# Expert layer of a decoder block: products with u kept on chip and gated from PSUM, v rows of two token tiles summed on TensorE strips

## The chip, the cores and the metric

The kernel runs on one core of a Trainium2 chip. A core has five engines that work side by side, each through its own instructions in order: TensorE (PE, matrix products into PSUM), VectorE (DVE), ScalarE (ACT), GpSimd (POOL) and SyncE (SP, which here only issues transfers). Sixteen DMA engines move data between DRAM and the on-chip memory SBUF; POOL issues the gathers by index, SP the plain transfers. The metric is the time of one execution in microseconds, the median of several runs.

## The reference

A block of a decoder with 512 tokens of 1024 values. Two token mixers (a gated linear recurrence and a dilated window attention) are merged and added to x; behind them comes the expert layer, which this change is about:

```python
def peer_ffn(x, w_q, sub_keys, u, v):
    q = (x @ w_q).reshape(B, S, PEER_HEADS, 2, PEER_HALF)
    s = jnp.einsum('bshpc,hpnc->bshpn', q, sub_keys)
    s1, i1 = lax.top_k(s[..., 0, :], PEER_TOPK)
    s2, i2 = lax.top_k(s[..., 1, :], PEER_TOPK)
    ...                                   # the best 16 of the 256 sums of each head
    gate = jax.nn.softmax(top_s, axis=-1)
    def block(args):
        xb, ib, gb = args
        hid = jnp.einsum('thkd,td->thk', u[ib], xb)
        a = jax.nn.gelu(hid, approximate=False) * gb
        return jnp.einsum('thk,thkd->td', a, v[ib])
```

Each token picks 128 of 16384 experts (8 heads of 16). For each picked expert the token's product with a row of u goes through gelu and a gate, and weighs a row of v; u and v have 16384 rows of 1024 float32 values, 67 MB each.

## The kernel before

The 512 tokens are four tiles of 128. The mixers run by halves (`Front(0)` for tiles 0 and 1, `Front(1)` for 2 and 3). `routing(T, rq)` finds a tile's 128 experts per token and their gates. The expert layer then reaches u and v in two ways.

*By gathering.* Tiles 0 and 3 (`UG`) gather their rows of u: for pair number j, one indirect transfer brings 128 rows, one for each token, and DVE reduces their product with the tokens' vector (L626, in `u_steps`). A tile needs 128 such gathers of 512 KB. Tile 3 also gathers its rows of v, and DVE adds each, weighted, to an accumulator (L645, in `v_steps`). The pool `gat` has three places for gathered rows (`row`), and two more (`rq`) take some of the later ones.

*By streaming.* Tiles 1 and 2 (`UD`) meet all of u: `hidden(b)` loads one of 128 blocks of 128 experts (`ub`), splits it into a high and a low part (`uh` on ACT, `ul` on POOL or DVE) and makes 24 products with 256 tokens (L109), then gelu. Tiles 1, 2 and 0 (`VD`) meet all of v in the last loop: block b's activations (`Gc`, split into `ah` and `al`) and its rows of v (`vb`, split into `vh` and `vl`) give 18 products of 128 x 512 (L834).

For the streamed tiles the gates have to be spread: `scatter_steps` builds from the pairs' two key numbers, by comparisons (`e12`, L666) and products (`eg`, L670) on DVE and small matrix products (L680), a 128 x 128 table of gates for each token, four tokens in a group. ACT copies it into `Gx`, and it goes to DRAM (`g_d`) ordered by tokens and comes back (`Gc`) by blocks. For tile 0 the scattered weights already hold gelu and gate; for tiles 1 and 2 the products with u are multiplied in when a block is used (L825).

The order of the work: the program's text gives priorities, and a scheduler orders each engine's instructions from them with its own model of time. Two pumps (`rows` and `scat`) put steps of gathering and scattering between other work, so many to a unit. 46 hidden blocks (`NPRE`) run ahead of the products with v; the other 82 run between them, in a ring of 58 places.

Of the kernel before, what the change touches and what calls it, by code (L numbers as in the profile page):

```python
# [18 lines left out]
P = 128  # L19
# [49 lines left out]
def kernel(ctx: ExitStack, tc: tile.TileContext, x, wst, par, cst, cols, g2, keys, u, v, ut, vr, out):  # L69
# [28 lines left out]
    def accumulate(out, ws, xs, cut, w_stays):  # L98
        """Sum over the blocks of w x, in three products where they come in two parts."""
# [24 lines left out]
    # lower bound: softmax over the two logit rows, row 0  # L124
# [5 lines left out]
    # values of the first group by token; of the other two with every fourth token's in a row  # L130
# [13 lines left out]
    class Front:  # L144
        """The mixers of one half of the tokens, and the queries of their expert layer."""

        def __init__(self, h, hi_pool, after_unit):
# [5 lines left out]
            for t in range(NT):  # L153
# [5 lines left out]
                for c in range(0, KC, 4):  # L159
# [20 lines left out]
        def slot(self, i, ks=slice(0, KC)):  # L180
            """Row blocks ks of a slot's weights, UK of them in a tile: the blocks' operands in order."""
# [14 lines left out]
        def proj(self, i, x, T):  # L196
            """A slot's 256 columns of the half's products with x, on the partitions (T) or along them."""
# [112 lines left out]
        def proj_attn(self):  # L310
# [47 lines left out]
            # with the scores' scale of 1 / 8  # L358
# [69 lines left out]
        def proj_gates(self):  # L428
# [6 lines left out]
            # behind the last exponential: the functions' tables take turns  # L435
# [5 lines left out]
        def post(self):  # L441
            """Merge, output projection, second norm and expert queries."""
# [22 lines left out]
            for b in range(4):  # L465
# [13 lines left out]
            for t in range(NT):  # L479
# [21 lines left out]
                # x1 waits in the output rows it belongs to  # L501
# [17 lines left out]
    def route_bank(T):  # L519
        pt = pvg.tile([P, 512], F32, name="vg") if T == 3 else pr.tile([P, 512], F32, name="pr")  # L520
# [11 lines left out]
    def routing(T, rq):  # L532
        """Top 16 of the 256 sums of the two halves' top 16.  A pair (a, b) has (a+1)(b+1)-1 pairs before it that
        are no worse, so only those with (a+1)(b+1) <= 16 can be among them."""
# [64 lines left out]
        if T in VD:  # L599
            pt = route_bank(T)  # L600
# [302 lines left out]
```

## Time and profile before

| | |
|---|---|
| time, median of 3 runs (lowest to highest) | 1847.26 us (1845.63 to 1848.25) |
| the profiled execution, first to last instruction | 1845.0 us |
| busy: PE, DVE, ACT, POOL | 91%, 78%, 43%, 43% |
| DMA, mean over the span | 475.61 MB, 258 GB/s |
| gathers by index | 384 of 512 KB |

The profile shows one execution. Busy times are shares of the span; a PE that is busy need not be at its peak, since products overlap in the array and each is shown with its whole way through it. A product of plain float32 shows as two records, one of the split operands (`uh`, `vh`, ...) as one. The granted clock is a share of TensorE's full speed, 1.00 or 0.50 at a time. The profiled execution's span is 2.3 us under the median.

### The profile page before, as it was taken

The page shows a single profiled execution, that of the slowest core. Times are in us where ns is not written, and L with a number is a line of the kernel's source. Part 1 is how long each engine was busy: PE and PEld are TensorE (multiplying, and loading weights), DVE is VectorE, ACT ScalarE, POOL GpSimd, SP SyncE. Part 2 cuts the span into 40 slices and gives each one's busy share as a digit, 9 for nine tenths or more (in the row PEclk, how much of TensorE's full clock was granted, in tenths as well). Part 3 has the DMA queues.
Part 4 walks back from the last instruction along what each step waited for, and adds up shares of the span by engine and source line. Part 5 has one row for each costly group of instructions (what it writes and reads, how often), then busy time and mean ns, then how long its engine had stood idle before and what let it go on. Part 6 is the DMA issues. An engine that isn't in the chain of part 4 may idle for free.

```text
span 1845.0 us, 28370 instructions
## 1 busy us (share of the span) xinstructions
PE 1674.0 (91%) x10573; PEld 1482.8 (80%) x10573; DVE 1444.1 (78%) x2681; ACT 795.6 (43%) x1348; POOL 793.6 (43%) x546
## 2 busy tenths in 40 slices
PE   6999889889789989888867899999999999999987
PEld 6998888667667878777867878888888888888766
DVE  5644547887887758999999977877877788888777
ACT  5655551211114556368756534343343434343232
POOL 3211312463664335556566543344323464444442
PEclk9999999988899989889978899999999999999999
DMA  6453553778787887534455799999988999999887
GB/s 196 153 158 119 175 194 118 270 235 276 244 279 264 297 298 261 183 111 145 152 183 202 238 372 334 339 328 326 367 298 299 345 339 341 340 340 317 288 309 278
DMA packets 169963, 475.61 MB, mean 258 GB/s; under 512 B 14304, under 2 KB 62688, under 8 KB 168800
## 3 DMA queue, kind: packets, MB, share of 16 engines
q1 hardware_dynamic: 112416, 270.56, 43.0%
q0 software_dynamic: 55296, 201.35, 30.9%
q10 hardware_dynamic: 2112, 1.88, 0.3%
q8 instruction: 83, 1.36, 0.3%
q14 instruction: 56, 0.46, 0.1%
HBM read 443.85 MB, written 28.84 MB: 256 GB/s over the span
## 4 chain that ended last, share of the span: by engine, by line
PE 47%; DVE 25%; DMA 11%; issue 9%; POOL 5%; ACT 1%; DVEq 0%; POOLq 0%; SPq 0%; ACTq 0%
PE acc L834 19%; PE pp L109 13%; PE ph L109 10%; DMA row<-in_u_dram,idx 6%; DVE row L626 4%; DVE e L666 4%; DVE eg L670 3%; POOL row L618 3%; DMA Gc<-g_d 3%; PE pg L680 2%; PE pr L680 1%; DVE cs L564 1%; DVE rest L515 1%; DVE ti L514 1%; DVE h2g L645 1%
## 5 line engine op out<-in xcount | busy, mean ns | idle before, releaser
L618 POOL DMA_INDIRECT row<-in_u_dram,idx x206 | 254.9, 1237 | 383.8 <-DVE row L626 274.3
L626 DVE SCALAR_TENSOR_TENSOR row<-row,h2g 128x1024 f32<-128x1024 f32 x206 | 272.4, 1328 | 62.2 <-DMA row<-in_u_dram,idx 61.3
L109 PE MATMUL ph<-hH,uh 128*128 128x256 f32 x1024 | 302.1, 295 | 7.1 <-ACT pre L792 6.0
L109 PE MATMUL ph<-hH,ul 128*128 128x256 f32 x1024 | 302.9, 296 | 5.0 <-POOL ul L95 5.0
L109 PE MATMUL ph<-hL,uh 128*128 128x256 f32 x1024 | 299.0, 292 | 0.0
L834 PE MATMUL acc<-vl,ah 128*128 128x512 f32 x768 | 241.8, 396 | 9.3 <-DVE vl L95 9.3
L834 PE MATMUL acc<-vh,al 128*128 128x512 f32 x768 | 240.0, 393 | 0.0
L94 ACT ACTIVATE uh<-ub 128x1024 fp32r<-128x1024 f32 x128 | 136.7, 1068 | 230.7 <-PE ph L109 214.1
L834 PE MATMUL acc<-vh,ah 128*128 128x512 f32 x768 | 222.5, 395 | 9.9 <-ACT vh L94 9.9
L109 PEld LDWEIGHTS ph<-hH,uh 128*128 128x128 f32 x1024 | 205.9, 201 | 12.8 <-ACT pre L792 7.8
L109 PEld LDWEIGHTS ph<-hH,ul 128*128 128x128 f32 x1024 | 205.5, 201 | 6.3 <-POOL ul L95 5.8
L109 PEld LDWEIGHTS ph<-hL,uh 128*128 128x128 f32 x1024 | 204.6, 200 | 3.8
L680 PEld LDWEIGHTS <-e 128*128 128x128 bf16 x1152 | 124.8, 119 | 73.4 <-DVE eg L670 65.4
L834 PEld LDWEIGHTS acc<-vl,ah 128*128 128x128 f32 x768 | 143.2, 190 | 40.0 <-DVE vl L95 11.8
L834 PEld LDWEIGHTS acc<-vh,ah 128*128 128x128 f32 x768 | 142.9, 190 | 38.2 <-ACT vh L94 10.5
L834 PEld LDWEIGHTS acc<-vh,al 128*128 128x128 f32 x768 | 145.5, 190 | 31.8
L94 ACT ACTIVATE ah<-Gc 128x384 fp32r<-128x384 f32 x128 | 66.9, 523 | 229.4 <-PE acc L834 226.7
L95 DVE TENSOR_TENSOR vl<-vb,vh 128x1024 fp32r<-128x1024 f32 x128 | 156.1, 1219 | 12.2 <-ACT vh L94 12.0
L618 POOL DMA_INDIRECT row<-in_v_dram,idx x76 | 111.6, 1469 | 120.0 <-DVE h2g L645 109.2
L680 PE MATMUL pg<-eg,e 128*128 128x128 bf16 x768 | 103.1, 297 | 51.8 <-DVE eg L670 51.3
L94 ACT ACTIVATE vh<-vb 128x1024 fp32r<-128x1024 f32 x128 | 135.6, 1059 | 28.6 <-DMA vb<-in_vr_dram 27.9
L674 ACT ACTIVATE eg<-e,pk 128x128 bf16<-128x128 bf16 x320 | 115.4, 565 | 70.9 <-DVE e L666 68.1
(279 smaller groups left out, 3582.4 us busy)
## 6 DMA issues: line engine op xcount, KB each, us to landing
w<-in_wst_dram SPq DMA_DIRECT2D x140, 512.0 KB
ub<-in_ut_dram SPq DMA_DIRECT2D x128, 512.0 KB
vb<-in_vr_dram SPq DMA_DIRECT2D x128, 512.0 KB
Gc<-g_d SPq DMA_DIRECT2D x15, 1536.0 KB
g_d<-Gx SPq DMA_DIRECT2D x16, 960.0 KB
g_d<-Gx SPq DMA_DIRECT2D x8, 1024.0 KB
row<-in_u_dram,idx POOLq DMA_INDIRECT x206
sc<-in_x_dram SPq DMA_DIRECT2D x4, 512.0 KB
```

What stands on the lines that cost most here:

```text
L94: nc.scalar.activation(hi, x, AF.Copy)
L95: (eng or nc.vector).tensor_tensor(out=lo, in0=x, in1=hi.bitcast(F32), op=ALU.subtract)
L109: nc.tensor.matmul(out, l, r, start=(i == 0), stop=(i == len(ops) - 1))
L514: nc.vector.max_index(out=ids[:, 0:8], in_max=vals[:, 0:8], in_values=src)
L515: nc.vector.match_replace(out=rest[:, :w], in_to_replace=vals[:, 0:8], in_values=src, imm_value=-BIG)
L618: nc.gpsimd.indirect_dma_start(out=r, out_offset=None, in_=src, in_offset=bass.IndirectOffsetOnAxis(ap=index, axis=0))
L626: nc.vector.scalar_tensor_tensor(r, r, 1.0, h2g[T], op0=ALU.mult, op1=ALU.mult, accum_out=hid[:, g, j:j + 1])
L666: nc.vector.tensor_tensor(out=e12, in0=iota[:, None].to_broadcast([P, 2, NKEY, GS]), in1=e[:, 0:2].to_broadcast([P, 2, NKEY, GS]), op=ALU. ...
L670: last_e2[0] = nc.vector.tensor_tensor(out=eg[:, :n], in0=e12[:, 1:2].to_broadcast([P, n, NKEY, GS]), in1=e[:, 2:2 + n].to_broadcast([P, n ...
L674: nc.scalar.activation(eg[:, 2, :, q], e12[:, 1, :, q], AF.Copy, scale=pk3[:, VD.index(T), i + k + q:i + k + q + 1])
L680: nc.tensor.matmul(pt[:, q], e12[:, 0, :, q0 + q], eg[:, j, :, q0 + q], start=(j == 0), stop=(j == 2))
L834: nc.tensor.matmul(acc[t][c], lt, r[:, c * 512:(c + 1) * 512], start=(b == 0 and i == 0), stop=(b == NKEY - 1 and i == 2))
```

## The change

Tile 0 leaves the streamed products with v: `VD` is gone, and the last loop has 12 products a block instead of 18, for tiles 1 and 2. Tiles 0 and 3 gather their rows of v, 256 gathers in place of 128. These now run by token: `idxT` holds the transposed indices, a gather brings the 128 rows of v of one token, and PE sums them with the token's weights: a column of weights stands in a strip of zeros (`wz`), so that a product of 32 columns adds one token's row to its place in PSUM (L653 of the new kernel). Tokens 32 apart go to the four strips of the array (`tile_position`), and a step of `v_steps` gathers two rows.

All 128 hidden blocks are done before the scatter, and their gelus stay in SBUF (`hid_all`, two tiles of 64 blocks). The scatter, now for tiles 1 and 2 only, multiplies its table from PSUM right onto them (L690 of the new kernel); `Gx`, `g_d`, `Gc` and the pump `scat` are gone. Then the products with v follow. The loads of u have two places instead of three, those of v four, in the places of `hH` and `hL`; gathered rows have five places in turn (`row_places`), from the second half's mixers on. POOL makes the low part of 16 blocks of u instead of 46.

```diff
 UG = (0, 3)
 UD = (1, 2)
-VD = (1, 2, 0)
...
+ROWS_F, ROWS_U, ROWS_S, ROWS_V = 3, 1.25, 1.5, 1.2
...
+        if T in UG:
+            nc.tensor.transpose(pt[:, 0], full, ident)
+            nc.vector.tensor_copy(idxT[:, UG.index(T)], pt[:, 0])
...
     def v_steps(T):
         g = UG.index(T)
-        acc = const.tile([P, D], F32, name="h2g")
-        for j in range(P):
-            r = row(idx[:, g, j:j + 1], v, j % 5 < 2)
...
-                nc.vector.scalar_tensor_tensor(acc, r, hid[:, g, j:j + 1], acc, op0=ALU.mult, op1=ALU.add)
-            yield 1
+        av = aT[:, g].rearrange("p (c m) -> p c m", c=NR)
+        acc = [pv.tile([P, 512], F32, name=f"pv{c}") for c in range(2)]
+        for m in range(RQ):
+            w = wz[m % len(wz)]
+            nc.scalar.activation(w[:, :, RQ - 1:RQ], av[:, :, m:m + 1], AF.Copy)
+            for c0 in range(0, NR, 2):
+                cc = range(c0, c0 + 2)
+                rs = [row(idxT[:, g, c * RQ + m:c * RQ + m + 1], v) for c in cc]
+                for h in range(2):
+                    for c, r in zip(cc, rs):
+                        nc.tensor.matmul(acc[h][c * RQ:(c + 1) * RQ], w[:, c, RQ - 1 - m:2 * RQ - 1 - m],
+                                         r[:, h * 512:(h + 1) * 512], start=(m == 0), stop=(m == RQ - 1),
+                                         tile_position=(0, c * RQ))
+                yield 2
+        finish(T, acc)
...
-                    nc.scalar.activation(Gx[:, :, k + q0:k + q0 + 4].rearrange("p i t -> p t i"), pt, AF.Copy)
...
-            nc.sync.dma_start(out=g_d[:, gi, k0:], in_=Gx[:, k0:])
...
+        t0 = ti * P + k
+        for i, a in enumerate(hid_all):
+            at = a[:, :, t0:t0 + GS]
+            nc.vector.tensor_mul(at, pt[:, :, i * HB:(i + 1) * HB].rearrange("p t i -> p i t"), at)
...
-    gat = ctx.enter_context(tc.tile_pool(name="gat", bufs=3, side="left", **TILE))
+    gat = ctx.enter_context(tc.tile_pool(name="gat", bufs=2, side="left", **TILE))
...
+    row_places = [(gat, "row", 2)] * 2 + [(rx, "rowx", 3)] * 3
...
+        for b in range(HB, NKEY):
+            hidden(b)
+            rows(ROWS_U)
+
+    with tc.tile_pool(name="gb", bufs=1, side="right", **TILE) as gb, \
+            tc.tile_pool(name="pg", bufs=3, space=PSUM, side="right", **TILE) as pg:
+        for k in range(0, P, GS):
+            for ti in range(len(UD)):
+                scatter(ti, k)
+                rows(ROWS_S)
...
     for b in range(NKEY):
-        if b % GB == 0:
...
-                nc.sync.dma_start(out=Gc, in_=g_d[:, :, b:b + GB])
-        a = pre[b]
-        gsl = Gc[:, :, b % GB]
-        nc.vector.tensor_mul(gsl[:, :ngu], a.rearrange("p (g t) -> p g t", t=GT), gsl[:, :ngu])
+        a = hid_all[b // HB][:, b % HB]
...
-        for t in range(len(VD)):
+        for t in range(len(UD)):
...
-        if b + NPRE < NKEY:
-            hidden(b + NPRE, ph)
-        rows(ROWS_D)
+        rows(ROWS_V)
```

Where the scheduler puts the instructions. First DVE behind the mixers, while the routings of the last tiles run. Before, the scatter's comparisons (`e`) and products (`eg`) stand between the routing's steps:

```order
L666 TENSOR_TENSOR e_6829<-iota,pk 128x1024
L551 CAST tf<-ti 128x128
L513 MAX sv<-cs 128x8 x4
L585 TENSOR_REDUCE idf<-sel 128x16
L670 TENSOR_TENSOR eg<-e_6829,pk 128x1024
L552 TENSOR_SCALAR tf<-tf 128x4x16
L514 MAX_INDEX si<-sv,cs 128x8
```

Now, at the same part of a routing, the subtractions `ul` and the products of gathered u rows (`row`, `rq`, `keys_sb` are their places) stand there:

```order
L92 TENSOR_TENSOR ul<-ub,uh 128x1024
L629 SCALAR_TENSOR_TENSOR keys_sb,hid<-keys_sb,h2g 128x1024
L629 SCALAR_TENSOR_TENSOR rq,hid<-rq,h2g 128x1024
L577 TENSOR_TENSOR eq<-iota,sf 128x800
L92 TENSOR_TENSOR ul<-ub,uh 128x1024
L629 SCALAR_TENSOR_TENSOR rq,hid<-rq,h2g 128x1024
L582 TENSOR_REDUCE idf<-sel 128x16
L629 SCALAR_TENSOR_TENSOR row,hid<-row,h2g 128x1024 x2
```

What moved: the scatter left this stretch of DVE, and between the first step of routing 3 and the transposing of tile 3's weights 140 products with u rows and 46 subtractions came in.

Then PE in the second half of the hidden blocks. Before, hidden products (`ph`) stood between the products with v (`acc00` to `acc21` are three tiles by two halves of the columns):

```order
L834 MATMUL acc10_9808<-vh_15453,ah_15447 128x512
L834 MATMUL acc11_9809<-vh_15453,ah_15447 128x512
L834 MATMUL acc20_9810<-vh_15453,ah_15447 128x512
L834 MATMUL acc21_9811<-vh_15453,ah_15447 128x512
L109 MATMUL ph_14355<-hH_68,uh_14351 128x256
L109 MATMUL ph_14355<-hL_69,uh_14351 128x256
```

Now the strips (`pv0` and `pv1` are the two halves of the columns) stand between the hidden products:

```order
L653 MATMUL pv0_6180<-row_11154,wz0_3086 32x512
L653 MATMUL pv1_6181<-row_11154,wz0_3086 32x512
L653 MATMUL pv0_6180<-rq_11156,wz0_3086 32x512
L653 MATMUL pv1_6181<-rq_11156,wz0_3086 32x512
L653 MATMUL pv0_6180<-rq_11186,wz1_3087 32x512
L653 MATMUL pv1_6181<-rq_11186,wz1_3087 32x512
L106 MATMUL ph_8910<-hH_68,uh_8906 128x256
L106 MATMUL ph_8910<-hL_69,uh_8906 128x256
L653 MATMUL pv0_6180<-keys_sb_11188,wz1_3087 32x512
L653 MATMUL pv1_6181<-keys_sb_11188,wz1_3087 32x512
L106 MATMUL ph_8910<-hH_68,ul_8907 128x256
```

What moved: the two halves of one row, which are one strip of the array, stand side by side, and the row of the next strip often only after some hidden products. Of the 256 rows of v, 24 stand among the first 62 hidden blocks, 145 among the other 66 (100 runs of strips, 71 of a single row, three of five rows) and 87 among the scatter (25 runs); none is left for the last loop.

Last, DVE in the scatter, where nothing else is left on it (`hid` with its numbers are the two tiles of gelus):

```order
L674 TENSOR_TENSOR e_11616<-iota,pk 128x1024
L678 TENSOR_TENSOR eg<-e_11585,pk 128x1024
L678 TENSOR_TENSOR eg<-e_11616,pk 128x1024
L690 TENSOR_TENSOR hid_5554<-pg,hid_5554 128x64x4
L690 TENSOR_TENSOR hid_8474<-pg,hid_8474 128x64x4
L674 TENSOR_TENSOR e_11648<-iota,pk 128x1024
```

What moved: the scatter is a stage of its own, behind all hidden blocks and ahead of all products with v, and two products from PSUM came to each group.

## Rows read from the trace of the kernel before

**Rows 1.** Windows: length; PE, PEld, DVE, ACT, POOL busy; clock; DMA share; GB/s.

```profile
0.00:295.00 295.00, 268.48 (x2305) 254.40 (x2306) 154.24 (x259) 152.47 (x250) 63.89 (x32) 0.98 0.50 157
295.00:690.00 395.00, 348.95 (x1899) 288.06 (x1898) 312.66 (x862) 121.48 (x265) 184.06 (x149) 0.91 0.78 263
690.00:1075.00 385.00, 311.73 (x2276) 293.25 (x2275) 359.25 (x773) 234.57 (x434) 226.98 (x139) 0.88 0.57 192
1075.00:1835.00 760.00, 744.33 (x4096) 646.96 (x4095) 615.67 (x787) 287.10 (x403) 318.65 (x227) 0.99 0.92 328
```

**Rows 2.** The page, part 3: queue, packets, MB, share of 16 engines' span.

```profile
q1 hardware_dynamic: 112416, 270.56, 43.0%
q0 software_dynamic: 55296, 201.35, 30.9%
```

**Rows 3.** The chain that ended last: start, duration in us, what, how many.

```profile
412.88 7.51 DMA row<-in_u_dram,idx
719.91 2.87 PE pr L680 x24
1113.24 4.13 PE acc L834 x18
1126.00 2.84 PE ph L109 x24
```

**Rows 4.** Lines 666 and 670 by source: shortest, median and longest in ns.

```profile
L666 DVE TENSOR_TENSOR e<-iota,pk x96: 660/686/3107, 567.5 to 1044.1; 128x1024 bf16<-128x1024 bf16 x96
L670 DVE TENSOR_TENSOR eg<-e,pk x96: 664/684/5904, 575.9 to 1047.0; 128x1024 bf16<-128x1024 bf16 x80, 128x1536 bf16<-128x1536 bf16 x16
```

**Rows 5.** Windows on lines 666, 670, 626 and 95, in this order.

```profile
295.00:690.00 395.00, 17.45 (x24) 0.91 0.78 263
690.00:1075.00 385.00, 86.33 (x72) 0.88 0.57 192
...
295.00:690.00 395.00, 17.08 (x23) 0.91 0.78 263
690.00:1075.00 385.00, 85.95 (x74) 0.88 0.57 192
...
295.00:690.00 395.00, 149.31 (x216) 0.91 0.78 263
690.00:1075.00 385.00, 63.26 (x88) 0.88 0.57 192
1075.00:1835.00 760.00, 126.35 (x208) 0.99 0.92 328
...
690.00:1075.00 385.00, 14.11 (x12) 110.92 (x44) 0.88 0.57 192
```

**Rows 6.** Timeline of PE: start, us, instruction; plain float32 products, full and in strips.

```profile
670.66 3.19 PE L109 MATMUL pp<-vs,w 128*128 128x256 f32 x14
...
556.21 1.12 PE L386 MATMUL pt<-kT,vs 64*32 64x128 f32 x16
557.26 0.79 PE L109 MATMUL pp<-hT,w 128*128 128x256 f32 x1
```

**Rows 7.** Windows around these products: the granted clock is third from the end.

```profile
556.00:558.00 2.00, 2.00 (x19) 1.19 (x19) 2.00 (x4) 0.00 (x0) 1.70 (x2) 0.50 0.27 33
671.00:673.50 2.50, 2.50 (x14) 2.19 (x13) 0.34 (x1) 1.49 (x2) 0.00 (x0) 1.00 1.03 416
```

**Rows 8.** Groups by line and form: count, busy us, mean ns, idle before.

```profile
L95 DVE TENSOR_TENSOR ul<-ub,uh 128x1024 fp32r<-128x1024 f32 x82 | 101.1, 1233 | 53.7 <-ACT uh L94 51.6 <-ACT ah L94 1.2 <-issue 0.7
L825 DVE TENSOR_TENSOR Gc<-pre,Gc 128x256 f32<-128x256 f32 x128 | 44.6, 417 | 45.2 <-DMA Gc<-g_d 45.2
L454 DVE TENSOR_TENSOR pairA<-pp,pairA 128x512 f32<-128x512 f32 x8 | 5.5, 686 | 6.6 <-PE pp L109 6.6
```

**Rows 9.** Waits from 295 to 690 us: in total, times, the longest.

```profile
POOL row L618 <- DVE row L626: 98.7, 36, 24.4
DVE row L626 <- DMA row<-in_u_dram,idx: 48.6, 33, 5.2
```

More of the change, by code (lines that the diff above doesn't have):

```diff
@@ L519, in route_bank @@
     def route_bank(T):
-        pt = pvg.tile([P, 512], F32, name="vg") if T == 3 else pr.tile([P, 512], F32, name="pr")
+        pt = pr.tile([P, 512], F32, name="pr")
         return pt.rearrange("p (n k) -> p n k", k=NKEY)
@@ L631, in u_steps @@
[L631 to L635 removed]
+            nc.scalar.activation(hid, hid, AF.Gelu)
+            nc.vector.tensor_mul(hid, hid, gates[:, T])
+            pt = pvg.tile([P, 512], F32, name="vg")
+            nc.tensor.transpose(pt[:, :P], hid, ident)
+            nc.vector.tensor_copy(aT[:, g], pt[:, :P])
@@ new lines, in scatter @@
+    def scatter(ti, k):
+        e = pk[:, ti, :, None, k:k + GS]
+        e12 = gb.tile([P, 2, NKEY, GS], BF16, name="e12", bufs=2)
+        nc.vector.tensor_tensor(out=e12, in0=iota[:, None].to_broadcast([P, 2, NKEY, GS]),
+                                in1=e[:, 0:2].to_broadcast([P, 2, NKEY, GS]), op=ALU.is_equal)
+        eg = gb.tile([P, 3, NKEY, GS], BF16, name="eg", bufs=2)
+        n = 2 if k // GS % 4 < ACT3 else 3
+        nc.vector.tensor_tensor(out=eg[:, :n], in0=e12[:, 1:2].to_broadcast([P, n, NKEY, GS]),
+                                in1=e[:, 2:2 + n].to_broadcast([P, n, NKEY, GS]), op=ALU.mult)
+        if n == 2:
+            for q in range(GS):
+                nc.scalar.activation(eg[:, 2, :, q], e12[:, 1, :, q], AF.Copy, scale=pk3[:, ti, k + q:k + q + 1])
+        pt = pg.tile([P, 512], F32, name="pg").rearrange("p (n k) -> p n k", k=NKEY)
+        for q in range(GS):
+            for j in range(3):
+                nc.tensor.matmul(pt[:, q], e12[:, 0, :, q], eg[:, j, :, q], start=(j == 0), stop=(j == 2))
+        t0 = ti * P + k
+        for i, a in enumerate(hid_all):
+            at = a[:, :, t0:t0 + GS]
+            nc.vector.tensor_mul(at, pt[:, :, i * HB:(i + 1) * HB].rearrange("p t i -> p i t"), at)
@@ L760 @@
     routing(1, rq1)
-    pr_bank = lambda: pr.tile([P, 512], F32, name="pr")
-    scat.add(scatter_steps(1, pr_bank))
     f.hgrn(0)
@@ L771 @@
         rows(2 * P)
-        scat(P)
     fctx.close()
-    dp = ctx.enter_context(tc.tile_pool(name="dp", bufs=1, side="right", **TILE))
-    us = ctx.enter_context(tc.tile_pool(name="us", bufs=2, side="right", **TILE))
-    pre = []
-    Gcs = [dp.tile([P, NGT, GB, GT], F32, name="Gc")]
-    nc.sync.dma_start(out=Gcs[0][:, :P // GT], in_=g_d[:, :P // GT, :GB])
-    def hidden(b, pool):
-        dst = dp.tile([P, NU], F32, name="pre", bufs=RING)
-        pre.append(dst)
-        ub = us.tile([P, KC, P], F32, name="ub", bufs=3)
+    pv = ctx.enter_context(tc.tile_pool(name="pv", bufs=1, space=PSUM, side="right", **TILE))
@@ L791, in hidden @@
         accumulate(pt, [tuple(a[:, k] for a in ubs) for k in range(KC)], (hH, hL), slice(None), True)
-        nc.scalar.activation(dst, pt, AF.Gelu)
-    with tc.tile_pool(name="php", bufs=2, space=PSUM, side="right") as php, \
-            tc.tile_pool(name="pg", bufs=3, space=PSUM, side="right") as pg:
-        pg_bank = lambda: pg.tile([P, 512], F32, name="pg")
-        routing(2, rq2)
-        scat.add(scatter_steps(0, pg_bank))
-        scat.add(scatter_steps(2, pg_bank))
-        scat(P)
-        for b in range(NPRE):
-            hidden(b, php)
-        routing(3, rq3)
@@ L804 @@
-    h2g[3] = const.tile([P, D], F32, name="h2g")
-    nc.sync.dma_start(out=h2g[3], in_=h2_d)
-    rows.add(u_steps(3))
-    with tc.issue_after(last_e2[0].ins):
-        rows(4)
-    rows.add(v_steps(3))
-    rctx.close()
-    ph = ctx.enter_context(tc.tile_pool(name="ph", bufs=1, space=PSUM, side="left", **TILE))
-    vs = ctx.enter_context(tc.tile_pool(name="vs", bufs=2, side="left", **TILE))
+        nc.scalar.activation(hid_all[b // HB][:, b % HB], pt, AF.Gelu)
+    v0 = v_steps(0)
+    rows.add(itertools.islice(v0, ROWS_V0 // 2))
@@ new lines @@
+    rows.add(u_steps(3))
+    rows.add(v0)
+    rows.add(v_steps(3))
+    with tc.tile_pool(name="us", bufs=2, side="right", **TILE) as us, \
+            tc.tile_pool(name="php", bufs=3, space=PSUM, side="right", **TILE) as php:
+        routing(3, rq3)
+        routing(2, rq2)
+        h2g[3] = const.tile([P, D], F32, name="h2g")
+        nc.sync.dma_start(out=h2g[3], in_=h2_d)
+        for b in range(HB):
+            hidden(b)
+            rows(ROWS_U)
+        rctx.close()
+        row_places[2:] = [(rq_pool, "rq", 2)] * 2 + [(rq_pool, "keys_sb", 1)]
+        hb = ctx.enter_context(tc.tile_pool(name="hb", bufs=1, side="left", **TILE))
+        hid_all.append(hb.tile([P, HB, NU], F32, name="hid1"))
+        for b in range(HB, NKEY):
+            hidden(b)
+            rows(ROWS_U)
@@ L835 @@
                                      start=(b == 0 and i == 0), stop=(b == NKEY - 1 and i == 2))
-        if b + NPRE < NKEY:
-            hidden(b + NPRE, ph)
-        rows(ROWS_D)
+        rows(ROWS_V)
     rows(2 * S)
-    for t, T in enumerate(VD):
-        x1r = gat.tile([P, D], F32, name="row")
-        nc.sync.dma_start(out=x1r, in_=out[T * P:(T + 1) * P])
-        for c in range(2):
-            cs = slice(c * 512, (c + 1) * 512)
-            nc.vector.tensor_add(x1r[:, cs], acc[t][c], x1r[:, cs])
-        nc.sync.dma_start(out=out[T * P:(T + 1) * P], in_=x1r)
+    for t, T in enumerate(UD):
+        finish(T, acc[t])
```

121 lines of the change are left out of this document (44 added, 77 removed).

## The prediction

> **What bounds the kernel now.** I read the windows by stage first. The profiled execution spans 1845.0 us (the median of the runs is 2.3 us above it), and it falls into four stages with different limits [rows 1]. To 295 us: the first half's mixers, PE busy 268 of 295. From 295 to 690: the second half's mixers with gathers of u beside them; no engine is full (PE 349, DVE 313 of 395), DMA at 0.78. From 690 to 1075: DVE busy 359 of 385, so DVE sets the pace, in a stage with the 46 hidden blocks that run ahead and 72 of the 96 groups of the scatter [rows 5]. From 1075 to 1835: PE busy 744 of 760 and DMA at 0.92 and 328 GB/s, both nearly full. The last 10 us store. So the 91% of PE in the table above is an average, and what PE could deliver is read from the chain: a block of 18 products with v takes 4.13 us, 0.229 each, and a block of 24 hidden products 2.84 us, 0.118 each [rows 3]. In the last stage 128 x 4.13 = 529 and the remaining 82 blocks x 2.84 = 233 give 762: that stage is PE at its peak, hardly a wait in it.
>
> The waits of the second stage show why it is loose: POOL waited 98.7 us for DVE to give back a place of a gathered row, and DVE 48.6 us for rows to land [rows 9]. A gather stands in the chain with some 7.5 to 8 us [rows 3]; three places allow no more.
>
> **The change, stage by stage.** I name the new stages A to G. A load is 524 kB (128 x 1024 x 4), gathered or streamed.
>
> A, the first half, keeps its order on every engine: **295**.
>
> B, the second half. Scatter leaves it: 17.5 + 17.1 us of DVE [rows 5]. Nine more rows come in (117 stand there, 108 did: 216 entries, two a row) at 149.3 / 108 = 1.38 us [rows 5]: +12. DVE falls from 313 to 291. On POOL it is the next gather that stands behind a place not yet given back, and DVE's products with u wait for that. Five places instead of three should take most of the 48.6 us; I take three quarters, so the 82 us of DVE idleness become 46. 291 + 46 = 337 is the lower end, 395 (nothing gained) the upper. 263 GB/s x 395 = 104 MB need 301 us at full rate (below), so transfers would not forbid it; at 0.9 full they seldom come without waits. I take **350**.
>
> C, the hidden blocks as long as u rows of tile 3 are reduced on DVE. The new order has 62 hidden blocks on PE up to the transposing of tile 3's weights, and on DVE both routings, 140 row products and 46 subtractions ul. From the old third stage: 359.3 - 86.3 - 86.0 (scatter) - 63.3 (rows) - 14.1 (halves) = 110 us are the routings and small things [rows 1, 5]. The rows cost 140 x 1.30; that is between 63.3 / 44 = 1.44 in that stage and 126 / 104 = 1.21 in the last [rows 5]. So 182, the subtractions 46 x 1.233 = 57 [rows 8]: 349. What lies between the median and the longest of the same scatter instruction (0.686 and 3.107 us [rows 4]) is worth a look: 72 of them took 1.20 on average here. It is the stage in which POOL runs subtractions of 110.9 / 44 = 2.5 us [rows 5], and those are 16 instead of 46 now. I add 30 for what is left of that. PE needs 62 x 2.84 = 176, transfers (62 + 152 rows) 112 MB. DVE ran at 93% in the old stage: 349 to 400, I take **380**.
>
> D, the other 66 hidden blocks, with 145 rows of v on PE. This is where the change is dear. One row is two products of 32 x 512, each in full float32. No such product is in the trace. Its bounds: a 128x256 float32 product shows as two records, and 14 records ran in 3.19 us at full clock. One alone takes 0.79 at half clock, some 0.39 at full; (3.19 - 0.39) / 13 = 0.215 from one to the next [rows 6, 7]. So 512 columns take 0.43 a record, and a row four records, 1.72 us, if nothing overlaps. Narrow strips do overlap: 16 records of 128 columns in 32-wide strips started at 556.21, and the next full product at 557.26, at a granted clock of 0.50 [rows 6, 7]. In series they would take 16 x 0.215 = 3.44 (half the columns at half the clock), they took 1.05, so four strips ran together, less 0.19 for draining. But the order on PE undoes the pairing: both halves of one row go to the same strip, and the scheduler puts hidden products between one row and the next. 100 runs of strips stand in D, 71 of them a single row. A run costs at least 1.72, and three runs of five rows cost twice that: 177 us; in series all 145 rows cost 249. The row is near the first, so I take 177. Each run begins and ends with a change of shape: 0.19 on leaving by the row above (at half clock), somewhat less at full; I take 0.25 for both, 25 us. 66 x 2.84 = 187. Sum 389, transfers 211 loads, 111 MB. In-order waits for rows come on top: **405**, bounds 365 and 470.
>
> The Trainium skill, "TensorEngine Tiling", Key Properties, says that changing the tiling mode drains the engine, while tiles of one mode run in parallel. The gap at 557.26 agrees. By parallel tiles alone D would be 365, by the drain at each of the 199 changes it is the sum above.
>
> E, the scatter by itself, 64 groups. DVE: e12 0.686, eg 0.684 [rows 4], or 1.03 where it has 1536 elements instead of 1024 (one of four), and two products from PSUM of 256 elements, 0.417 each if they run like the one from SBUF, 0.686 each if the scattered reading costs as much as twice the elements [rows 8]. 2.29 to 2.83 a group, 147 to 181 us. PE: 12 x 0.119 [rows 3] = 1.43 a group, 25 runs of strips with 52 us, 150 in all. The 87 rows: five places, a cycle of 7.5 us in flight and some 3 us of issue and use, 2.1 a row, 183. Three limits close together: **185**, bounds 160 and 260 (the latter with strips at half clock, as at 556).
>
> F, the products with v, now for two tiles and with nothing beside them: 12 x 0.229 = 2.74 a block, 351, with the first load **355**. DVE, 616 of 760 us busy there before [rows 1], loses u's rows, v's sums and ul from this stage; transfers are 67 MB. G, the end: **10**.
>
> Taken out at no cost: the 50 MB of gates through DRAM (25 MB written and read; transfers were full only where PE was too), DVE's accumulation of v, ACT's copies to Gx. They are hidden by PE in the old last stage; where PE is no cover (the third stage) they are counted above.
>
> Sum: 295 + 350 + 380 + 405 + 185 + 355 + 10 = 1980, against 1845; with the 2 us to the median **1982**. PE is given 351 instead of 529 us of products with v, but 250 of strips, and the work that once lay under PE's last stage, the scatter and u's rows on DVE, now stands before it in line.
>
> **Rivals.** *Slower still: strips do not overlap.* If runs go in series, D rises to 470 and E, with 150 us of strips, to 250: about 2110. The 16 records speak against it; that two halves of one row share a strip speaks for some of it. The same price comes if the clock drops: the old third stage had 0.88 [rows 1].
>
> *B gains nothing*, since transfers or the mixers' own order hold it: 2027. For it: 0.78 of DMA already.
>
> *Faster: C and D run at the pace of transfers.* 297 rows and 128 blocks are 223 MB. Full rate by the queues: 270.6 MB in 43.0% and 201.4 MB in 30.9% of 1845 us [rows 2], 341 and 353, taken as 346 GB/s: 644 us instead of 785. That gives 1841, and it decides from there: C and D must stay under 650 us together. For it: the old last stage ran 760 us at 0.92. Against it: the least counts, 349 on DVE and 365 on PE, are 714 one after the other, and the order on each engine lets neither overlap.
>
> The Trainium skill, "DMA: Bandwidth & Descriptors", Bandwidth, puts the limit of HBM at about 358 GB/s for each core and that of the fabric, for a core alone, at 435. The queues' 346 agree with the first. By the second, at 425 as measured there, the transfers of C and D would take 524 us, and this rival would come to 1721.
>
> **How the numbers follow.** The sum (1900 to 2060) 0.70; strips in series or clock down (2060 to 2200) 0.13; between the sum and the transfers' pace (1851 to 1900) 0.10; transfers' pace or better 0.07, of which 0.02 within 0.2% (3.7 us, about what a measurement of this kernel tells from nothing) and 0.05 faster. All lower ends together give 1869, all upper ends 2194. From 1875 to 2100 leaves out less than 2 in 10.
>
> **What would show it.** Right: hidden products that begin by 650; DVE over 90% busy to about 1025, then under 30% for 400 us while PE is full with strips of 0.8 us in chain; a scatter stage of 160 to 260 us; a last stage of 128 blocks at 2.74 with DMA near 0.55. Wrong: D under 340, which would mean strips overlapping across hidden products; a second half still of 395; a C in which DVE waits for rows.

## The result, and the profile after

The changed kernel takes **2040.3 us** (median; 2030.7 to 2041.9) against 1847.2: a ratio of 1.1044, 95% interval 1.1019 to 1.1068. The forecast was slower, 1982 us, 1875 to 2100. The profiled execution spans 2028.9 us. Its windows, cut where the named stages end in this trace (for each engine busy us and instructions, then the granted clock as a share of 2.4 GHz, the DMA share and GB/s):

```profile
0.00:295.00 295.00, 268.59 (x2307) 254.47 (x2308) 154.30 (x260) 152.76 (x250) 64.44 (x34) 0.97 0.48 157
295.00:645.00 350.00, 314.30 (x1705) 257.15 (x1703) 311.67 (x921) 76.67 (x160) 219.59 (x171) 0.97 0.88 316
645.00:1028.00 383.00, 273.65 (x1622) 231.87 (x1622) 327.52 (x752) 94.42 (x143) 275.33 (x199) 0.83 0.83 293
1028.00:1447.00 419.00, 403.65 (x2162) 233.69 (x2163) 80.64 (x71) 95.25 (x167) 149.97 (x141) 1.00 0.76 261
1447.00:1673.00 226.00, 197.71 (x1125) 110.75 (x1117) 129.40 (x258) 73.94 (x216) 86.68 (x86) 0.90 0.65 219
1673.00:2029.00 356.00, 350.21 (x1536) 289.49 (x1536) 213.40 (x261) 187.41 (x254) 0.00 (x0) 0.99 0.60 186
```

| stage | forecast | measured |
|---|---|---|
| A, first half | 295 | 295 |
| B, second half | 350 | 350 |
| C, hidden blocks beside u rows | 380 | 383 |
| D, hidden blocks beside v strips | 405 | 419 |
| E, scatter | 185 | 226 |
| F and G, products with v, end | 365 | 356 |
| span | 1980 | 2029 |

Where [rows 1] had one stage with PE and DMA both full, there are now three in line, each with room on a different engine: PE in C (274 of 383 us busy), DVE in D (81 of 419), transfers in F (0.60). The chain that ended last in D (followed back from the last instruction through what released each one), by line:

```profile
by line: PE ph L106 45.2%; PE pv L653 42.5%; DMA keys_sb<-in_v_dram,idxT 6.2%; issue 2.4%; ACT uh L91 2.2%; POOL rq L621 0.9%; DVE ul L92 0.3%; POOL row L621 0.2%; ACT wz L647 0.1%; ACTq L91 0.0%; POOLq L621 0.0%; ACTq L647 0.0%
```

Of 419 us that is 189 of hidden products (forecast 187), 178 of strips (forecast 177) and 26 of waits for a row. PE's timeline in D shows what a run of strips costs, that is, strips with no other product between them (start, us, count; x8 is two rows, x4 one):

```profile
1240.20 1.92 PE L653 MATMUL pv<-rq,wz 128*32 128x512 f32 x8
1242.05 0.39 PE L106 MATMUL ph<-hH,uh 128*128 128x256 f32 x1
1242.27 0.28 PE L106 MATMUL ph<-hL,uh 128*128 128x256 f32 x1
1242.48 1.91 PE L653 MATMUL pv<-keys_sb,wz 128*32 128x512 f32 x4
1244.31 0.39 PE L106 MATMUL ph<-hH,ul 128*128 128x256 f32 x1
```

Two rows cost what one costs: 1.85 us to the next hidden product against 1.83. Over all records of D, 100 runs hold 144 rows and take 210 us from first strip to next product: 2.1 us a run. The Trainium skill, "TensorEngine Tiling (Array Packing)", Key Properties, has tiles of one mode working in parallel and a drain at a change of mode; the trace agrees with the first (1.85 beside 1.83), and the second is small here (four records of 0.43 are 1.72 of the 1.83).

### The profile page after: what moved, and what is told of

It reads as the page before. It is cut to its first block, busy times and chain, and to the rows that moved or that the text cites. A ratio compares the mean times of both kernels' runs of the same rounds, so it can differ in the third digit from the quotient of the medians.

```text
span 2028.9 us, 27909 instructions
## 1 busy us (share of the span) xinstructions
PE 1808.1 (89%) x10446; PEld 1377.4 (68%) x10446; DVE 1216.9 (60%) x2515; ACT 680.4 (34%) x1189; POOL 796.0 (39%) x630
## 4 chain that ended last, share of the span: by engine, by line
PE 60%; DVE 18%; DMA 7%; issue 6%; POOL 5%; ACT 1%; DVEq 0%; POOLq 0%; ACTq 0%
PE acc L836 17%; PE pv L653 13%; PE ph L106 12%; PE pp L106 12%; DVE rowx L629 5%; PE pg L686 3%; DVE row L629 2%; DMA rowx<-in_u_dram,idx 2%; DMA keys_sb<-in_v_dram,idxT 2%; POOL row L621 2%; DMA row<-in_v_dram,idxT 1%; DVE ul L92 1%; DVE rest L512 1%; DVE rq L629 1%; DMA w<-in_wst_dram 1%
## 5 line engine op out<-in xcount | busy, mean ns | idle before, releaser
L92 DVE TENSOR_TENSOR ul<-ub,uh 128x1024 fp32r<-128x1024 f32 x112 | 138.3, 1248 | 335.8 <-ACT uh L91 335.6
L653 PE MATMUL pv<-row,wz 128*32 128x512 f32 x416 | 181.4, 603 | 5.3 <-DMA row<-in_v_dram,idxT 4.9
L621 POOL DMA_INDIRECT row<-in_v_dram,idxT x104 | 109.6, 1054 | 183.3 <-PE pv L653 149.2
L791 ACT ACTIVATE hid<-ph 128x256 f32<-128x256 f32 x128 | 48.6, 379 | 367.7 <-PE ph L106 367.6
L621 POOL DMA_INDIRECT rowx<-in_u_dram,idx x110 | 137.5, 1250 | 74.6 <-DVE rowx L629 30.5
L629 DVE SCALAR_TENSOR_TENSOR rowx<-rowx,h2g 128x1024 f32<-128x1024 f32 x110 | 150.8, 1377 | 22.4 <-DMA rowx<-in_u_dram,idx 18.1
L621 POOL DMA_INDIRECT row<-in_u_dram,idx x102 | 125.4, 1230 | 90.3 <-DVE row L629 57.4
L629 DVE SCALAR_TENSOR_TENSOR row<-row,h2g 128x1024 f32<-128x1024 f32 x102 | 139.8, 1375 | 31.1 <-DMA row<-in_u_dram,idx 31.1
L621 POOL DMA_INDIRECT rq<-in_v_dram,idxT x92 | 98.7, 1073 | 122.2 <-PE pv L653 107.9
L653 PE MATMUL pv<-rq,wz 128*32 128x512 f32 x368 | 142.4, 599 | 3.6 <-DMA rq<-in_v_dram,idxT 3.6
L836 PE MATMUL acc<-vh,ah 128*128 128x512 f32 x512 | 138.0, 391 | 1.0 <-ACT ah L91 1.0
```

Source lines behind the costliest of these rows:

```text
L92: (eng or nc.vector).tensor_tensor(out=lo, in0=x, in1=hi.bitcast(F32), op=ALU.subtract)
L621: nc.gpsimd.indirect_dma_start(out=r, out_offset=None, in_=src, in_offset=bass.IndirectOffsetOnAxis(ap=index, axis=0))
L629: nc.vector.scalar_tensor_tensor(r, r, 1.0, h2g[T], op0=ALU.mult, op1=ALU.mult, accum_out=hid[:, j:j + 1])
L653: nc.tensor.matmul(acc[h][c * RQ:(c + 1) * RQ], w[:, c, RQ - 1 - m:2 * RQ - 1 - m], r[:, h * 512:(h + 1) * 512], start=(m == 0), stop=(m = ...
L791: nc.scalar.activation(hid_all[b // HB][:, b % HB], pt, AF.Gelu)
L836: nc.tensor.matmul(acc[t][c], l[:, t * P:(t + 1) * P], r[:, c * 512:(c + 1) * 512], start=(b == 0 and i == 0), stop=(b == NKEY - 1 and i = ...
```

## Experiments

Beside each median stands its ratio to the kernel before, run on the same chip.

**Pairs.** Hold the four products of two rows together, to see whether the order of strips is D's price.

```diff
+                (c, r), (c1, r1) = zip(cc, rs)
+                first = strip(c1, r1, 0)
+                with tc.issue_after(first.ins):
+                    strip(c, r, 0)
+                    strip(c1, r1, 1)
+                    strip(c, r, 1)
```

> The four products of a pair of v rows are held together on PE, the later row's first. Read from the changed kernel: 71 runs of one row took 1.83 us each, 16 runs of two rows 1.85 as well. Theory (strips of two rows overlap when they stand together, and PE sets the pace beside the hidden blocks): the stage with 64 hidden blocks and 107 rows has 64 x 2.84 + 54 x 1.85 = 282 us of PE and takes 290 to 330 instead of 419; the 32 rows that the order moves into the last stage add 16 x 1.85 = 30 there; the kernel comes to 1935 to 1975. Rival (row places and landing pace the rows, PE only waits inside its strips): rows go on at the 2.9 us that 145 rows took in 419 us, the stage takes 107 x 2.9 = 310 but PE is idle in a fifth of it, the scatter stage stays at 226, and with longer waits for the second row of each pair the kernel stays above 1990.

1967.5 us, 1.0654 (1.0626 to 1.0682). The window of D:

```profile
1045.00:1350.00 305.00, 290.40 (x1970) 205.77 (x1970) 78.29 (x66) 91.55 (x153) 120.57 (x107) 0.99 0.84 295
```

50 runs for 107 rows now, 100 us: again 2.0 a run, 0.93 a row instead of 1.46. PE is still busy 290 of 305 us and the kernel is under 1990, as the first theory has it; the length alone would not tell, since the rival had 310. Not all of D's 114 us are gained: 37 rows fewer stand in it, and the last stage, which got 33 of them, took 385 instead of 356. The chain of this D goes through gathers and their places, no longer through products:

```profile
by line: issue 40.5%; DMA rq<-in_v_dram,idxT 21.3%; DMA keys_sb<-in_v_dram,idxT 14.9%; POOL rq L621 7.3%; POOL row L621 6.3%; POOL keys_sb L621 3.2%; PE ph L106 3.0%; DMA row<-in_v_dram,idxT 2.0%; PE pv L652 1.3%; POOLq L621 0.3%; PE vg L63
```

So the price of a run is shown, and the row places come close behind it.

**Strips undone.** v rows gathered by pair number again, one row for each token, as before the change (the expectation's "by token" is a slip), and summed on DVE; all else of the change stays.

```diff
+            r = row(idx[:, g, j:j + 1], v)
+                nc.vector.scalar_tensor_tensor(acc, r, hid[g][:, j:j + 1], acc, op0=ALU.mult, op1=ALU.add)
```

> The strips undone: v rows are gathered by token, as before the change, and summed on DVE with one scalar_tensor_tensor each, for both tiles; gates from PSUM, products kept on chip, row places and everything else as changed. Theory (strips on PE are the dear part, 2.0 us of PE for a row where DVE has 340 us idle beside the last 66 hidden blocks): that stage has 159 rows x 1.35 + 67 x 1.28 = 300 us of DVE, 66 x 2.84 = 187 of PE and 226 loads, 118 MB, 342 us; it takes 330 to 360 instead of 419; the stage ahead grows by some 15 rows (400), the scatter has 129 + 66 x 1.35 = 218 us of DVE and takes 225 to 245, the last stage 355: 1965 to 2005. Rival (where a row is summed matters little, because transfers and row places pace the rows): no stage moves by over 15 us, 2025 to 2055.

1929.7 us, 1.0437 (1.0395 to 1.0479), lower than the range, mostly by E. D and E:

```profile
1032.00:1371.00 339.00, 250.02 (x1606) 235.68 (x1606) 279.05 (x230) 92.16 (x135) 221.50 (x159) 0.85 0.95 349
1371.00:1574.00 203.00, 101.11 (x768) 83.67 (x768) 202.08 (x322) 73.04 (x196) 79.41 (x68) 0.51 0.57 184
```

D runs at the transfers' rate (349 GB/s, 0.95), E has DVE busy throughout. More than half of the loss, 111 of 193 us, is what summing on strips costs over summing on DVE. The 349 stands beside the 358 GB/s for a core that the Trainium skill gives ("DMA: Bandwidth & Descriptors", Bandwidth).

**Three places in B.** Rows go round three places until the mixers end, then five.

```diff
-    row_places = [(gat, "row", 2)] * 2 + [(rx, "rowx", 3)] * 3
+    row_places = [(gat, "row", 2)] * 2 + [(rx, "rowx", 3)]
...
+    row_places[2:] = [(rx, "rowx", 3)] * 3
     fctx.close()
```

> Rows gathered in the second half's mixers go round three places instead of five; five again from the hidden blocks on. Theory (the second half fell from 395 to 350 us because five places took away waits for rows): hidden blocks begin 30 to 50 us later, at 675 to 695, and since the order moves the rest of tile 0's u rows beside the hidden blocks, that stage grows too; 2055 to 2100 for the kernel. Rival (the second half is shorter because the scatter's work left it): hidden blocks begin within 10 us of 645, DVE's waits for rows in that stage stay near the 26 us that they have now, and the kernel is within 15 us of 2040.

2055.7 us, 1.1120 (1.1089 to 1.1150): at the low edge of the theory's total, but not by its mechanism, and neither side whole. The first hidden products, of the changed kernel, of this one, and of the kernel before (first and last start behind the durations), and DVE's largest wait in this one's B:

```profile
L106 PE MATMUL ph<-hH,uh x1024: 277/282/582, 644.9 to 1445.3; 128*128 128x256 f32 x171
```
```profile
L106 PE MATMUL ph<-hH,uh x1024: 274/282/582, 651.0 to 1441.1; 128*128 128x256 f32 x171
```
```profile
L109 PE MATMUL ph<-hH,uh x1024: 274/281/582, 687.1 to 1718.5; 128*128 128x256 f32 x171
```
```profile
DVE row L629 <- DMA row<-in_u_dram,idx: 48.2, 25, 6.2
```

The 48.6 us of [rows 9] are back, and hidden products still begin at 651. So the two places gave 6 of the 42 us from 687 to 645, and moved 22 rows (106 to 128) into B. The rest came with what else the change took out of it. The scatter is the likely part: beside its 35 us on DVE it held PE, in B of the kernel before, for 34 us (first PE, then PEld; its products' line 680), and PE's busy time there fell from 349 to 314:

```profile
295.00:690.00 395.00, 33.80 (x264) 30.03 (x264) 0.91 0.78 263
```

No run puts the scatter alone back, so this is argued, not shown.

**Half of u's products.**

```diff
+            n = D // 2 if T else D
+            nc.vector.scalar_tensor_tensor(r[:, :n], r[:, :n], 1.0, h2g[T][:, :n], op0=ALU.mult, op1=ALU.mult,
```

> Leaves out half of the product with u for tile 3: DVE multiplies and sums 512 of 1024 columns of each gathered row; the gathers are whole. Theory of the prediction (the first 62 hidden blocks stand under DVE's row products): DVE loses 128 x 0.65 = 83 us of the 328 that it is busy in that stage, which falls from 383 us to the transfers' 325 to 340; the kernel comes to 1980 to 2005. Rival (five row places and the way of a gather, not DVE, set 2.5 us a row): the stage stays at 370 to 385, and the kernel at 2025 to 2045.

2046.4 us, 1.1085 (1.1038 to 1.1133). C alone:

```profile
653.00:1011.00 358.00, 268.00 (x1601) 224.99 (x1602) 266.77 (x747) 93.03 (x141) 243.37 (x198) 0.85 0.87 309
```

DVE lost 61 us and C 25: neither theory whole. DVE sets part of C's pace; what holds the other part is not shown (no engine is full, transfers at 0.87). The total kept nothing of it: the new order put 152 rows instead of 144 into D, in 119 runs (236 us) instead of 100, and D took 455.

**Eight places in E; rows spread over E.** Two kernels, both with 2.3 rows asked for at each hidden block (that alone was not run).

```diff
+        row_places += [(gb, "rowg", 3)] * 3
```
```diff
+                last = scatter(ti, k)
+                with tc.issue_after(last.ins):
+                    rows(ROWS_S)
```

> Eight row places instead of five in the scatter stage alone (and 2.3 rows asked for with each hidden block, so that the rows traced there are those that run there). Theory from the changed kernel's trace (while rows run, PE is busy 95% of the time: 48 groups at 1.46 and 87 rows at 1.2 in series; then 16 groups alone at 2.67): places do not matter, the stage has 64 x 1.46 + 83 x 1.2 = 193 us of PE and takes 195 to 225 instead of 226; the kernel comes to 2010 to 2040. Rival, as the prediction put it (five places and a cycle of 10.5 us set 2.1 us a row): the rows come at 1.3 us, DVE is the limit with 64 x 2.67 = 171, the stage takes 170 to 180, and the kernel comes to 1975 to 1990.

> Strips in the scatter stage are queued on PE behind the scatter products of the group with which they are traced, and 2.3 rows are asked for with each hidden block, so that 88 rows spread over all 64 groups instead of the first 48. Theory (the changed kernel's 16 groups without rows, 43 us at a granted clock of 0.57, are a rest that the prediction's three limits side by side did not have): PE has 64 x 1.46 + 88 x 1.2 = 199 us, the stage takes 200 to 210 instead of 226, the kernel 2015 to 2030. Rival (PE and DVE hand each group to and fro, so the stage takes the sum of waits wherever the rows stand, as in the paired kernel, where rows were spread and the stage took 222 us with PE busy 187): 218 to 230, and 2035 to 2050.

2048.3 us, 1.1095 (1.1060 to 1.1130), and 2059.9, 1.1153 (1.1111 to 1.1195). E took 205 and 220 us; D grew to 453 and 445 (118 and 115 runs), which ate it. Strips alone in E, of the changed kernel, with eight places, and spread (first PE, then PEld):

```profile
1447.00:1673.00 226.00, 104.71 (x357) 25.04 (x349) 0.90 0.65 219
```
```profile
1485.00:1689.00 204.00, 68.89 (x332) 16.77 (x332) 0.83 0.62 222
```
```profile
1479.00:1698.00 219.00, 97.89 (x352) 19.01 (x352) 0.94 0.63 210
```

With eight places 83 rows were done 150 us into E (1.81 us each), not 88 in 183 (2.08), their strips took 69 us of PE, not 105, and 54 us of scatter alone came after them instead of 43. Spread out, no rest was left, but 88 rows stood in 47 runs, at 2.1 us each 99 us, and the time hardly fell. So neither theory for E holds alone: more places quicken the rows, and rows in many short runs cost PE as much as rows that land one by one.

**Rows of u and v in turn**, unpaired and paired (first queued 24 v, 128 u, 104 v; now two u, two v).

```diff
-    rows.add(itertools.islice(v0, ROWS_V0 // 2))
-    rows.add(u_steps(3))
-    rows.add(v0)
+    def mixed(us3, v0):
+        for k in us3:
+            yield k
...
+        yield from v0
+    rows.add(mixed(u_steps(3), v_steps(0)))
```

> Rows of u of tile 3 and of v of tile 0 are queued in turn (two u, two v) instead of 24 v, 128 u, 104 v, so that 110 hidden blocks, not 62, stand beside the rows on DVE; the blocks ask for 2.3 rows each instead of 1.25. Nothing is left out. Theory of the prediction (the change loses because DVE's stage of 383 us and PE's of 419 stand one after the other): together they approach the transfers' pace, 297 rows and 128 blocks, 223 MB at 346 GB/s = 644 us; I expect 660 to 720 for both instead of 802, and 1885 to 1950 for the kernel. Rival (both stages are held by the five row places, 2.5 us a row in the first and 2.9 in the second): 290 rows at 2.7 give 780, and the kernel stays at 2000 to 2030.

> Both edits together: the products of two v rows held together on PE, and rows of u of tile 3 queued in turn with rows of v of tile 0. Beside rows on DVE stand 123 hidden blocks and 126 v rows. Theory (the first test showed the strips to be PE's excess: with rows in turn but unpaired, PE was busy 573 of 661 us, 110 x 2.84 + 127 rows at 2.05): PE is left with 123 x 2.84 + 63 x 1.85 = 466, DVE with some 430, and the transfers bind, 388 loads, 203 MB at 346 GB/s = 588 us; I expect 600 to 650 for this stage, some 25 for the last 5 blocks, 222 for the scatter as in the paired kernel, 372 for the last stage: 1885 to 1930. Rival (five row places pace the rows at 2.5 us, whatever PE does): 254 + 8 rows x 2.5 = 655 to 680 and 1935 to 1965, the gain of pairing alone.

2017.4 us, 1.0933 (1.0897 to 1.0969), and 2014.1, 1.0882 (1.0816 to 1.0947). The unpaired one's stage beside u rows and the rest of its hidden blocks, 780 us together:

```profile
653.00:1314.00 661.00, 573.24 (x3192) 382.66 (x3189) 392.53 (x795) 162.62 (x262) 383.51 (x302) 0.95 0.82 289
1314.00:1433.00 119.00, 112.09 (x580) 63.88 (x579) 23.18 (x21) 25.71 (x45) 40.31 (x38) 1.00 0.73 246
```

The paired one's long stage, and PE's waits in it (us, times, longest):

```profile
653.00:1373.00 720.00, 550.28 (x3489) 412.99 (x3488) 396.14 (x807) 180.94 (x287) 380.76 (x301) 0.90 0.79 275
```
```profile
PE ph L106 <- ACT uh L91: 46.6, 30, 11.6
PE ph L106 <- DVE ul L92: 40.9, 32, 3.9
PE pv L652 <- DMA row<-in_v_dram,idxT: 35.5, 11, 8.6
```

Here my theory fell. Unpaired, 780 us and 2017 are what the rival had. Paired, nothing is full, PE 550, DVE 396 of 720, DMA 0.79, and a row takes 2.84 us, slower than either side. Pairing brought 73 us with strips apart from u rows and nothing here. The lines suggest why: a strip that waits on PE for its second row holds up hidden products, and a landed v row waited 14 us (mean, gathers and strips matched in order) for its turn, in its place. Whether more places would help a queue with strips was not run.

**Rows of v where there is room.** DVE sums, but only some 112 v rows in D, 24 in E, 110 in F (there queued behind the block's last subtraction, low[-1]); then the same with u and v in turn; the same with 32 subtractions on POOL; and in turn with four places.

```diff
-ROWS_F, ROWS_U, ROWS_S, ROWS_V = 3, 1.25, 1.5, 1.2
+ROWS_F, ROWS_U, ROWS_S, ROWS_V = 3, 1.98, 0.35, 0.9
...
-        rows(ROWS_V)
+        with tc.issue_after(low[-1].ins):
+            rows(ROWS_V)
```
```diff
-UPOOL = 16
+UPOOL = 32
```
```diff
+    row_places[2:] = [(rx, "rowx", 3)] * 2
```

> v rows summed on DVE, as in the run before, and placed by hand: some 112 beside the last hidden blocks instead of 159, 24 instead of 66 in the scatter (each queued on DVE behind its group's first comparison) and 110 instead of 20 in the last stage, behind that block's subtraction. Nothing is left out. Theory (the last stage alone has DVE and transfers to spare: 213 of 350 us busy, 187 GB/s; every row taken out of the stages ahead gives its price back): the hidden stage has 179 loads, 94 MB = 271 us, DVE 112 x 1.28 + 67 x 1.25 = 227, and takes 275 to 300 instead of 339; the scatter 175 to 190 instead of 204; the last stage 213 + 110 x 1.28 = 354 us of DVE beside 351 of PE, 355 to 375; 1860 to 1895 in all. Rival (rows behind subtractions hold up PE in the last stage, which had no slack on PE): the last stage grows by 50 us or more, and the kernel stays above 1900.

> As the run beside it, and rows of u of tile 3 queued in turn with rows of v of tile 0, so that 111 hidden blocks stand beside both. Theory (what made the change slow is work in line that could lie beside other work): beside the 128 blocks DVE has 110 + 128 x 1.4 + 114 x 1.28 + 111 x 1.25 = 574 us, the transfers 369 loads, 193 MB at 346 GB/s = 559, PE 364; both parts together take 600 to 645 instead of 675 to 700, and the kernel comes to 1800 to 1840, under the kernel before the change. Rival (five row places, not DVE or transfers, pace a mixed queue, as when strips stood in it: 2.8 us a row): 242 rows x 2.8 = 680, no gain on the run beside it, 1860 to 1895.

> As the first of these runs, with 32 instead of 16 blocks' subtractions on POOL. Theory of the prediction (POOL's subtractions lengthen what DVE does beside them, 30 us for 16): DVE is rid of 16 x 1.25 = 20 us beside the u rows, and loses 30 more by longer rows; mean row product there rises from 1.40 to 1.6 us, and the stage grows by 5 to 20 us. Rival (POOL's help is worth its price): rows stay within 0.08 us of 1.40, the stage shrinks by 15 to 20.

> The mixed queue with late rows, with four row places instead of five beside the hidden blocks and in what follows; the rows of each stage are within five of those of that kernel, in which 242 rows beside 128 blocks took 691 us, 2.85 each. Theory (five places pace the mixed queue: each row holds a place from its gather's issue until its own turn on DVE): the pace goes up by 5/4 to 3.6 us, the stage to 840 to 870 us, the kernel to 1990 to 2020. Rival (DVE's 597 busy us and the order on it pace the queue, places have room): the stage grows by less than 40 us, 1840 to 1880. In between, the places would set the pace of part of the stage.

| kernel | us | ratio to before | interval |
|---|---|---|---|
| late rows | 1852.1 | 1.0030 | 1.0013 to 1.0047 |
| late rows, u and v in turn | **1840.6** | **0.9963** | 0.9946 to 0.9979 |
| late rows, 32 on POOL | 1871.0 | 1.0141 | 1.0112 to 1.0170 |
| in turn, four places | 1845.1 | 0.9984 | 0.9957 to 1.0011 |

The windows of C to F with late rows, and of C with D, E and F in turn:

```profile
627.00:1023.00 396.00, 262.49 (x1580) 244.29 (x1579) 367.90 (x845) 94.65 (x141) 289.55 (x198) 0.80 0.79 284
1023.00:1323.00 300.00, 236.31 (x1626) 224.57 (x1625) 220.16 (x182) 92.27 (x135) 157.87 (x113) 0.88 0.85 316
1323.00:1489.00 166.00, 100.35 (x772) 84.52 (x770) 154.36 (x280) 73.10 (x196) 26.61 (x23) 0.53 0.28 89
1489.00:1840.00 351.00, 350.13 (x1536) 289.23 (x1536) 329.38 (x370) 187.92 (x254) 98.38 (x103) 1.00 0.93 346
```
```profile
631.00:1322.00 691.00, 494.55 (x3196) 461.98 (x3195) 586.99 (x1024) 187.12 (x274) 445.69 (x310) 0.85 0.83 299
1322.00:1484.00 162.00, 100.41 (x768) 84.19 (x768) 154.05 (x283) 73.41 (x197) 26.88 (x23) 0.51 0.28 91
1484.00:1835.00 351.00, 350.33 (x1536) 289.19 (x1536) 329.39 (x370) 187.87 (x254) 98.44 (x103) 0.99 0.93 346
```

F took 108 row sums and not one microsecond more: DVE 329, transfers 346 GB/s, PE 350 of 351. That is the old last stage's balance again, and the late rows bring 78 us, more than forecast (1860 to 1895). Taking u and v in turn brought 5 us in the stage, not the 60 expected (DVE busy 587 of 691), and 12 in the median; what holds that stage is open. Strips undone, rows late and rows in turn lead from 2040 back to 1841: 6 us under the kernel before, which at a bar of 2% is the same time. With four places the stage is over at 1313, and E follows:

```profile
631.00:1313.00 682.00, 491.90 (x3198) 461.43 (x3196) 573.75 (x1010) 187.74 (x274) 437.12 (x299) 0.85 0.83 294
1313.00:1487.00 174.00, 100.62 (x772) 84.47 (x770) 163.73 (x293) 73.47 (x196) 34.72 (x31) 0.54 0.35 117
```

251 row products in 682 us stand against 260 in 691 with five, 2.72 against 2.66 us a row, not 3.6; E, which got the others, grew from 162 to 174. So row places do not set the pace, in this queue at least. POOL's price, by row products of the same shape while POOL subtracts and afterwards (last two numbers ahead of the idle time: busy us, mean ns), in the kernel with 32:

```profile
L631 DVE SCALAR_TENSOR_TENSOR rowx<-rowx,h2g 128x1024 f32<-128x1024 f32 x38 | 69.9, 1851 | 6.5 <-DMA rowx<-in_u_dram,idx 6.5
```
```profile
L631 DVE SCALAR_TENSOR_TENSOR rowx<-rowx,h2g 128x1024 f32<-128x1024 f32 x35 | 49.7, 1423 | 5.1 <-DMA rowx<-in_u_dram,idx 5.1
```

Those means mix rows beside POOL's arithmetic with others. Sorted by what POOL ran at the same time, in C of this kernel, 22 row products beside a subtraction took 2.78 us on average, 93 beside none of its arithmetic 1.21 (80 of them beside the issuing of a gather). Over all rows the mean rose from 1.38 to 1.55. C grew by 27 us (423 for 396), over the 5 to 20 forecast, though DVE lost 16 subtractions; PE's waits for POOL's subtractions rose too, from 47 to 81 us, so not all of it is DVE's:

```profile
631.00:1054.00 423.00, 266.68 (x1585) 246.42 (x1584) 383.30 (x825) 95.43 (x141) 328.16 (x212) 0.78 0.76 265
```

The Trainium skill, "SBUF — State Buffer", Terms, says that VectorE and GpSimd share a pair of ports under an exclusive lock, the loser blocking for a whole instruction; the longer rows agree in direction, no run here shows the lock.

## Why the prediction was right, and where it was off

**A, F, G.** As forecast: F's 128 blocks at 350 / 128 = 2.73 us, DMA 0.60.

**B: number right, reason wrong.** "Five places instead of three should take most of the 48.6 us" failed. They took 22 of these us (48.6 to 26), but B ends when the mixers do, and that moved from 687 to 651 with three places and to 645 with five. The scatter's leaving, which I had charged as 35 us of DVE and not as 34 of PE, is likely most of the rest. That 350 came out is luck.

**C: right, in part by luck.** 383 for 380; the rows took 180 us for the 182 forecast, but 128 of them at 1.40 instead of 140 at 1.30, two errors that cancel. DVE was busy 86%, not over 90, and waited little for rows (27 us). Half of u's products away brought 25 of 61 us, so DVE is a part of C's pace and not all. The 30 us for POOL's subtractions are of the right kind: in this C 7 row products beside one took 3.35 us, 26 beside POOL's other arithmetic 1.61, the rest 1.21, together 25 us more.

**D: right in its mechanism.** 419 for 405: strips 178 in the chain for 177, hidden products 189 for 187, waits for rows 26 where I had allowed 16. The 25 us for changes of shape were too many: 1.83 a run less 1.72 is 0.11, 11 us for 100 runs; issue and the splitting of u took up the rest. A run costs the same with one row or two, in five kernels 2.0 to 2.1 us, and pairing took a row from 1.46 to 0.93: that was the mechanism.

**E: the step that was mis-sized.** 226 for 185, 41 of the 49 us by which the sum was off. "Three limits close together: 185" took the longest of DVE, PE and rows as the stage, and PE's limit was too low: "25 runs of strips with 52 us" were 26 runs that held PE for 105 (the line above), so PE was busy 198 us, not 150. The 52 let three to five rows of a run overlap. In the trace 40 of the 88 rows began on PE at their own landing, one after another, and runs of three rows took 3.5 us, of five 5.9 (medians); with eight places 7 of 83 began so, and the strips took 69. Two windows of E:

```profile
1580.00:1630.00 50.00, 48.46 (x272) 25.99 (x272) 27.66 (x55) 14.06 (x42) 22.55 (x23) 1.00 0.77 261
1630.00:1673.00 43.00, 24.58 (x196) 21.72 (x192) 31.81 (x65) 17.77 (x47) 0.00 (x0) 0.57 0.15 50
```

The rows kept their forecast pace: the last strip starts at 1630, 183 us into E, with PE 95% busy until then. But the order had put them beside the first 48 groups; 16 groups came after, 43 us at 2.7. The order on PE had that to read: I did not count the groups behind the last row. That E takes 162 to 166 us with late rows (24 rows, on DVE) and still 220 with 88 strip rows spread over it says that strips cost E some 55 us in both orders: they do not hide because PE, with them, is the fullest engine there. Why E is still 26 us longer than PE's 193 with rows spread stays open.

**Rivals.** Strips in series: seen inside each row (both halves in one strip), not between adjacent rows that have both landed. Transfers' pace: of C and D, D alone reached it, and only with the strips gone, 349 GB/s. The profiled execution was the fastest of five (2030.7 us), so the stages' sum stands 11 us under the median, where 2 were allowed.

## What to carry to other kernels

A change that takes bytes and products away can still lose if it turns work beside a full engine into work in a line: sum the stages, each by its own fullest engine. Ask what else stands beside each stage and which engine it leaves idle; here 108 row sums were moved into a stage whose DVE (213 of 356 us) and transfers (0.60) had room, and it grew by nothing. For small products between large ones, count the runs in the order, not the rows, ask whether the rows of a run will have landed together, and count what is left behind the last of two interleaved kinds of work.

## What was not expected of the hardware

- Two rows' strips (8 records) take 1.85 us, one row's (4 records) 1.83: adjacent strips of different columns overlap wholly if both rows have landed, the two halves of one row not at all.
- In the queue of u and v in turn, taking one of five landing places away took a row from 2.66 to 2.72 us, though a row stands in its place for its whole way from issue to use.
- A row product on DVE took 2.78 us beside a subtraction on POOL and 1.21 beside the issuing of a gather on POOL, as without it.
- PE with 128 blocks of products, DVE with 108 row sums and 346 GB/s of transfers ran side by side at 350 us, the time of the products alone.
